# A SwiGLU feed-forward on one core: first sums of two or three weight pairs made by adding transfers, results kept in the slots of the sums

## The chip, the cores and the metric

The kernel runs on one core of a Trainium2 chip. The metric is device time in microseconds (us), the median of several runs; the lower the better. The engines are named as in the profile: PE is TensorE (matmuls; PEld is the loading of its weights, which overlaps them), DVE is VectorE, ACT is ScalarE, POOL is GpSimd and SP is SyncE. SP issues most of the transfers, POOL some of them. Data lies in HBM, is worked on in SBUF (128 partitions), and TensorE adds its products up in PSUM, in eight banks of 128 x 512 fp32.

## The reference

A decoder layer on 256 tokens of width 2048: a normalised input goes through one input projection into two groups of heads, their outputs through an output projection, and a SwiGLU feed-forward of width 5632 follows. The change touches the last step alone:

```python
def hybrid_layer(x, ..., w_out, ffn_norm_g, w_gate, w_up, w_down):
    ...
    h = x + jnp.concatenate([gla_out, nsa_out], axis=-1) @ w_out
    m = rms_norm(h, ffn_norm_g)
    return h + (jax.nn.silu(m @ w_gate) * (m @ w_up)) @ w_down
```

Here w_gate and w_up are 2048 x 5632, w_down is 5632 x 2048, all fp32.

## The kernel before

**Precision.** A product of fp32 matrices is made of three matmuls of a reduced format (fp32r): each operand is split into a high part and a low part, and high x high, high x low and low x high are added in PSUM. The split of a weight tile (`in_parts`, L660 ff) is one ScalarE instruction for the high part (L661) and one VectorE instruction for the low part (L662).

**Blocks and pairs.** The feed-forward runs over 11 blocks of 512 columns. For a block `fb`, `gate_up(fb)` multiplies the normalised tokens (two tiles of 128) with the block's columns of w_gate and w_up. The 2048 rows of these go in eight *pairs* of 128-row tiles, a and b. A plain pair is 8 products of 128 x 128 by 128 x 512, so 24 matmuls. The other kind of pair does with 7 products (21 matmuls), by Strassen's method in Winograd's form on the 2 x 2 scheme of (tokens 0, tokens 1) x (a, b) x (gate, up). A pair with 7 needs:
- three weight tiles as they are (gate a, gate b, up a), split in one go as a 128 x 1536 tile; a plain pair splits four (128 x 2048);
- a *first sum* `s1` (two tiles: gate b + up b, and up a + up b; one VectorE instruction of 128 x 1024, L1210) and a *second sum* `s2` (two tiles made from `s1`; two VectorE instructions of 128 x 512, L1211 and L1212), each then split as 128 x 1024;
- *forms* of the tokens (`pair_forms`), made once for all blocks.

The products add up in PSUM banks numbered 1 to 8. At a block's end VectorE combines them (L1238 to L1241 after a copy by ScalarE, then L1252, L1255 and L1256 with the gate's activation on ScalarE) into five result tiles `q1, u, q5u, q7u, q57u`. Bank 8 is written by plain pairs alone.

**The order of the blocks.** Block 0 is followed straight by block 1. From there on, the down product of a block (`down`, 96 matmuls) stands between the gate and up products of later blocks: `gate_up(2)`, `down(1)`, and so on, so that a block's results have the time of a down product to be turned and split. Within a block the tiles of a pair are split ahead of the matmuls that use them, and a scheduling layer places the instructions of each engine; each engine then runs its own in order.

**Where a sum comes from.** `SUMS` names pairs whose sums are made earlier, in the projection stage, as background work (`sum_rows`), and kept in DRAM. `fetch_sums` (L1168) brings them back by two POOL transfers of 512 KB, one pair ahead. For those pairs VectorE makes no sum in the block. Before the change, blocks 2 to 7 have seven pairs with 7 products and pair 6 plain, one stored pair (7); blocks 8 to 10 have eight pairs with 7 products, three of them stored (2, 5, 7).

**Slots.** Tiles come from pools of a fixed number of slots; a new tile waits until the slot's last reader is done. `g4` is the common pool of 24 slots, `fsum` holds second sums (two slots), `fraw` the weights as loaded (three slots), `ftwo` split weights (four slots), and `f2` the block results and the work tiles of the forms (six slots).

Of the kernel before, what the change touches and what calls it, by code (L numbers as in the profile page):

```python
# [8 lines left out]
F32 = mybir.dt.float32  # L9
# [6 lines left out]
P = 128  # L16
# [21 lines left out]
def kernel(  # L38
# [182 lines left out]
    done = set()  # L221
    cols = kp.tile([P, 164], F32, name="cols")
    pc = bank()
    have_rows = transpose(pc[:, 0:16], rows0[:16, :], 16)
    have_cols = nc.vector.tensor_copy(cols[:, 0:16], pc[:, 0:16])
    ag, fg, gains = cols[:, 0:16], cols[:, 16:32], cols[:, 32:36]
    cw = cols[:, 36:100].rearrange("p (i c) -> p i c", i=4)
    pos = cols[:, 100:164].rearrange("p (w j) -> p w j", w=2)
    kgain = cp.tile([P, 3], F32, name="kgain")
# [6 lines left out]
    def cols_rest():  # L236
        for _ in range(8):
            yield
        nc.gpsimd.memset(w2b, 0.0)
        with behind(last["dma"]):  # L240
            small_loads()
        for _ in range(20):
            yield
        pc = bank()
        transpose(pc[:, 0:P], rows2)
        transpose(pc[:, P:P + 20], rows[:20, :], 20)
        nc.vector.tensor_copy(cols[:, 36:164], pc[:, 0:P])
        nc.vector.tensor_copy(cols[:, 16:36], pc[:, P:P + 20])
        TS(kgain, gains[:, 1:4], gains[:, 0:1], None, ALU.mult)
        third_group(w2r, w2b, slice(32, 64))  # L250
        done.add("cols")
# [779 lines left out]

    ALL7 = 8
    FIRST7.update({f: (0, 1, 2, 3, 4, 5, 7) for f in range(2, ALL7)})

# [6 lines left out]

    def pair_forms(pair, v):


        f = g2([4, P])
        a0, a1, b0, b1 = v[:, 0, :P], v[:, 0, P:], v[:, 1, :P], v[:, 1, P:]
        TT(f[:, 0], b1, a1, ALU.subtract)
        TT(f[:, 1], f[:, 0], b0, ALU.subtract)
        TT(f[:, 2], b0, b1, ALU.subtract)
        TT(f[:, 3], a0, f[:, 1], ALU.add)  # L1050
        r = forms[pair] = g4([2, 4, P], F32R)
        in_parts(r[:, 0], r[:, 1], f)

    def late_forms():
        for pair in PAIRS7:
            if pair not in EARLY7:
                for _ in range(6):
                    yield
                v, ks = g2([2, S]), slice(2 * pair % 4, 2 * pair % 4 + 2)
                with behind(last["d"]):  # L1060
                    TT(v, f32(hT_h[pair // 2][:, ks]), f32(hT_l[pair // 2][:, ks]), ALU.add)
                    pair_forms(pair, v)

# [30 lines left out]

    SUMS = {f: (2, 5, 7) if f >= ALL7 else (7,) for f in range(2, NFB)}
    SUMS[1] = (2, 3, 4, 5)
# [26 lines left out]
    def ffn_pools():  # L1123
        nonlocal g2, small
        for pool in (wp, s2p, s1p, cp):
            pool.release()
        fr = ctx.enter_context(tc.tile_pool(name="fr", bufs=1, reuse_waits="tile"))
        fs = ctx.enter_context(tc.tile_pool(name="fs", bufs=1, reuse_waits="tile"))
        fp = ctx.enter_context(tc.tile_pool(name="fp", bufs=1, reuse_waits="tile"))
        fw["sum"] = slot(fs, "fsum", 2)  # L1130
        fw["raw"], fw["two"] = slot(fr, "fraw", 3, LINE), slot(fp, "ftwo", 4, LINE)
        g2, small = slot(fs, "f2", 6), slot(fs, "fm", 4)

# [35 lines left out]


    banks = {}

    def gate_up(fb):
# [11 lines left out]

        order, sevens = (ORDER0, ORDER1, ORDER)[0 if fb == 0 else 1 if fb < ALL7 else 2], FIRST7.get(fb, PAIRS7)
        last7 = max(sevens, key=order.index)
# [6 lines left out]
        for at, pair in enumerate(order):  # L1194
# [6 lines left out]
            if at < 7:  # L1201
                fetch_sums(fb, order[at + 1])
            r = load4([(w_gate[0], a, 2, fb * FB), (w_up[0], a, 1 if ready else 2, fb * FB)])
            if ready:
                s1, s2 = fetched.pop((fb, pair))
            if pair in sevens:
                w = parts_of(r[:, 0:3])
                if not ready:
                    s1, s2 = g4([2, 512]), fw["sum"]([2, 512])
                    TT(s1, r[:, 1:3], r[:, 3:4].to_broadcast([P, 2, 512]), ALU.add)  # L1210
                    TT(s2[:, 0], s1[:, 1], r[:, 1], ALU.add)  # L1211
                    TT(s2[:, 1], s2[:, 0], r[:, 0], ALU.add)  # L1212
# [22 lines left out]
            if pair == last7:  # L1235
                q1, u, q5u, q7u, q57u = (g2([512]) for _ in range(5))
                act(q1, banks[1], AF.Copy)
                TT(u, banks[6], q1, ALU.add)  # L1238
                TT(q5u, banks[5], u, ALU.subtract)
                TT(q7u, banks[7], u, ALU.add)  # L1240
                TT(q57u, banks[5], q7u, ALU.subtract)  # L1241
                if fb == 1:
                    urgent.append(turn_act(0, (1, 5)))
                if fb:
                    seed(0, DOWN[min(fb - 1, 1)])
# [15 lines left out]
    def turn_act(fb, qs):  # L1261
# [13 lines left out]
        if fb == NFB - 1:  # L1275
            for pair in range(2):
                yield
                yield
                v, ks = g2([2, S]), slice(2 * pair, 2 * pair + 2)
                TT(v, f32(hi[:, ks]), f32(lo[:, ks]), ALU.add)  # L1280
                pair_forms(8 + pair, v)

# [24 lines left out]
    def down_last():  # L1307
# [56 lines left out]
        ws = parts_of(load4([(w_down[0], 4 * f, 4, 1536)]))  # L1364
        q1, u, q5u, q7u, q57u = (g2([512]) for _ in range(5))
        act(q1, at[1], AF.Copy)
# [79 lines left out]
```

## Time and profile before

| what | value |
|---|---|
| median of 3 runs | 1097.95 us (1097.88 to 1098.21) |
| the profiled execution, its own time | 1100.68 us |
| its span, first to last instruction | 1098.9 us |
| granted TensorE clock | 1.00 |
| ACT busy | 755.4 us (69%) |
| matmuls of gate and up products (L1179) | 1842 recorded, 431.3 us busy |
| transfers on POOL's queue | 46.14 MB, 11.4% of 16 engines' span |
| transfers on SP's queue | 223.68 MB, 59.2% |

The profile is one execution, some us longer than the median run; a difference that the trace shows is set against the profiled execution's own time. "Busy" is the time in which an engine ran instructions. A group row gives the line, engine, operation, names (output<-inputs), shapes and count, then busy time and the mean of one, then the idle time before its instructions and what ended it.

### The profile page before, as it was taken

What the parts mean: (1) busy time and instruction counts of PE and PEld (TensorE: products, weight loads), DVE (VectorE), ACT (ScalarE), POOL (GpSimd) and SP (SyncE); (2) the same over time, 40 slices, a digit from 0 to 9 for tenths busy, and PEclk for the clock granted to TensorE, in tenths of its full rate; (3) what the DMA queues carried; (4) which work ended last, traced back from release to release, by engine and by line L of the source; (5) the groups of instructions that cost most, each with busy time, mean ns of one, the idle gap of its engine ahead of it and who ended that gap; (6) DMA issues with size and microseconds to landing.
All of it is one profiled execution on the core that took longest, in us unless ns stands there. A gap on an engine that the chain in (4) does not pass through costs nothing.

```text
span 1098.9 us, 14699 instructions
## 1 busy us (share of the span) xinstructions
PE 1092.1 (99%) x5274; PEld 899.8 (82%) x5274; DVE 993.4 (90%) x1313; ACT 755.4 (69%) x1048; POOL 79.8 (7%) x150
## 2 busy tenths in 40 slices
PE   9999999999999999999999999999999999999998
PEld 8888888987888877888878888888888888888887
DVE  5778879986899888997999999999999999999997
ACT  7755557545687587666585866768585867777785
POOL 4100001032110100100000000000000000000000
PEclk9999999999999999999999999999999999999999
DMA  7999978467877956685566657576566768677663
GB/s 278 356 371 355 378 248 296 165 226 283 307 276 253 336 183 232 226 324 172 181 231 210 213 199 252 180 253 208 209 230 205 252 216 287 212 263 235 226 230 115
DMA packets 128885, 271.22 MB, mean 247 GB/s; under 512 B 7126, under 2 KB 9210, under 8 KB 128812
## 3 DMA queue, kind: packets, MB, share of 16 engines
q1 hardware_dynamic: 115532, 223.68, 59.2%
q0 software_dynamic: 12672, 46.14, 11.4%
q8 instruction: 41, 0.67, 0.2%
q10 hardware_dynamic: 608, 0.47, 0.1%
q14 instruction: 32, 0.26, 0.1%
HBM read 247.19 MB, written 23.07 MB: 246 GB/s over the span
## 4 chain that ended last, share of the span: by engine, by line
PE 82%; DVE 8%; issue 4%; ACT 3%; POOL 2%; DMA 1%; SPq 0%; DVEq 0%; POOLq 0%; ACTq 0%
PE bank L297 39%; PE bank L1179 36%; PE bank L215 2%; PE bank L1320 2%; DVE lo L145 2%; DVE ftwo L662 1%; DMA g<-in_x_dram 1%; PE bank L977 1%; ACT hi L144 1%; POOL sm L218 1%; DMA fraw<-in_w_up_dram 1%; ACT g L912 1%; DVE g L1111 0%; DVE g L1210 0%; POOL sc L218 0%
## 5 line engine op out<-in xcount | busy, mean ns | idle before, releaser
L1179 PE MATMUL bank<-ftwo,g 128*128 128x512 f32 x1842 | 431.3, 393 | 0.5 <-ACT ftwo L661 0.2
L1179 PEld LDWEIGHTS bank<-ftwo,g 128*128 128x128 f32 x1842 | 341.0, 188 | 77.9 <-DVE ftwo L662 5.0
L297 PE MATMUL bank<-hi,g 128*128 128x512 f32 (+1 forms) x1088 | 320.9, 376 | 0.4 <-ACT g L912 0.4
L662 DVE TENSOR_TENSOR ftwo<-fraw,ftwo 128x1536 fp32r<-128x1536 f32 (+1 forms) x130 | 256.6, 1976 | 8.2 <-ACT ftwo L661 7.4
L661 ACT ACTIVATE ftwo<-fraw 128x1536 fp32r<-128x1536 f32 (+1 forms) x130 | 216.0, 1664 | 28.3 <-DMA fraw<-in_w_up_dram 18.6
L297 PE MATMUL bank<-ftwo,g 128*128 128x512 f32 x960 | 220.6, 390 | 0.0
L297 PEld LDWEIGHTS bank<-hi,g 128*128 128x128 f32 x1088 | 191.6, 188 | 30.9 <-issue 1.0
L297 PEld LDWEIGHTS bank<-ftwo,g 128*128 128x128 f32 x960 | 179.6, 188 | 38.4 <-ACT bank L1291 0.3
L297 PE MATMUL bank<-lo,g 128*128 128x512 f32 (+3 forms) x544 | 193.0, 375 | 0.1
L144 ACT ACTIVATE hi<-raw 128x1024 fp32r<-128x1024 f32 (+3 forms) x124 | 130.7, 1059 | 81.9 <-PE bank L297 62.7
L145 DVE TENSOR_TENSOR lo<-raw,hi 128x1024 fp32r<-128x1024 f32 (+3 forms) x124 | 150.2, 1218 | 33.5 <-ACT hi L144 32.9
L661 ACT ACTIVATE ftwo<-g 128x1024 fp32r<-128x1024 f32 x76 | 80.3, 1057 | 75.1 <-DVE g L1210 48.9
L297 PEld LDWEIGHTS bank<-lo,g 128*128 128x128 f32 x544 | 98.3, 189 | 14.6 <-DVE lo L145 0.3
L662 DVE TENSOR_TENSOR ftwo<-g,ftwo 128x1024 fp32r<-128x1024 f32 x76 | 92.7, 1220 | 10.5 <-ACT ftwo L661 10.5
L662 DVE TENSOR_TENSOR ftwo<-fsum,ftwo 128x1024 fp32r<-128x1024 f32 x76 | 92.6, 1219 | 0.5 <-ACT ftwo L661 0.5
L661 ACT ACTIVATE ftwo<-fsum 128x1024 fp32r<-128x1024 f32 x76 | 79.6, 1048 | 5.4 <-DVE fsum L1212 3.7
L1303 ACT COPY g<-bank 128x512 f32<-128x512 f32 x80 | 46.0, 589 | 38.3 <-PE bank L297 36.7
L1210 DVE TENSOR_TENSOR g<-fraw 128x1024 f32<-128x1024 f32 x54 | 65.2, 1219 | 0.8 <-DMA fraw<-in_w_up_dram 0.8
L1291 ACT COPY bank<-g 128x512 f32<-128x512 f32 x80 | 45.3, 594 | 15.0 <-DVE f L1240 8.4
L661 ACT ACTIVATE g<-bank 128x512 fp32r<-128x512 f32 x46 | 27.2, 598 | 30.2 <-PE bank L215 24.3
L1168 POOL DMA_DIRECT2D g<-sums x20 | 10.6, 533 | 502.0 <-DVE ftwo L662 473.4
L215 PE MATMUL bank<-ident,g 128*128 128x128 f32 (+3 forms) x232 | 42.8, 278 | 1.3 <-DVE g L863 0.9
(250 smaller groups left out, 918.5 us busy)
## 6 DMA issues: line engine op xcount, KB each, us to landing
fraw<-in_w_gate_dram SPq DMA_DIRECT2D x86, 512.0 KB, 3.9
fraw<-in_w_down_dram SPq DMA_DIRECT2D x42, 1024.0 KB, 5.0
raw<-in_w_in_dram SPq DMA_DIRECT2D x36, 1024.0 KB, 5.8
fraw<-in_w_up_dram SPq DMA_DIRECT2D x66, 512.0 KB, 4.8
sums<-g POOLq DMA_DIRECT2D x40, 512.0 KB, 6.5
raw<-in_w_out_dram SPq DMA_DIRECT2D x16, 1024.0 KB, 8.6
g<-in_w_gate_dram SPq DMA_DIRECT2D x20, 512.0 KB, 8.4
g<-in_w_up_dram SPq DMA_DIRECT2D x20, 512.0 KB, 9.3
```

Of the source, the lines that this page charges most:

```text
L144: act(h[:, i:i + n], r[:, k + i:k + i + n], AF.Copy)
L145: last["d"] = TT(o[:, i:i + n], r[:, k + i:k + i + n], f32(h[:, i:i + n]), ALU.subtract)
L215: return nc.tensor.transpose(o, i, ident[:n, :n])
L218: nc.gpsimd.tensor_tensor(o, i, mhalf[:i.shape[0], :i.shape[1]], ALU.pow)
L297: last["mm"] = mm(bk[t], a[:, k, t * P:(t + 1) * P], ws[k][m][:, off:off + w], start=(first_ and k == 0 and i == 0), stop=(end and k == 3 ...
L661: act(hi, ps, AF.Copy)
L662: last["d"] = TT(lo, ps, f32(hi), ALU.subtract)
L1179: mm(banks[q], x, m, start=todo[q] == total[q], stop=todo[q] == 1)
L1210: TT(s1, r[:, 1:3], r[:, 3:4].to_broadcast([P, 2, 512]), ALU.add)
L1291: last["seed", n] = nc.scalar.copy(banks[qs[n][t]], h_sb[n][:, t, :])
L1303: nc.scalar.copy(h_sb[n][:, t, :], bs[t])
L1320: mm(bk, u, m, start=(first and i == 0), stop=(end and i == 2), skip_group_check=onto)
```

## The change

- In blocks 2 to 7 pair 6 becomes a pair with 7 products too, and the natural order of pairs is used in all blocks from 2 on. No block from 2 on writes bank 8 in its gate and up products.
- `SUMS` stores pairs 4 and 7 for blocks 2 to 7, pair 7 alone for blocks 8 to 10: 20 pairs in all with blocks 0 and 1, as many as before.
- `HALVES`: the first sum of pairs 2 and 6 (blocks 2 to 7) or 2, 4 and 6 (blocks 8 to 10) is made by transfers: POOL loads gate b and up a (256 KB each) into the two halves of a tile of the common pool, and a third transfer adds up b to both halves (512 KB). `fetch_half` is called two pairs ahead. VectorE then makes the second sum alone, and SP loads three tiles of the pair in place of four.
- The first sum that VectorE still makes goes to a slot of `fsum`, no longer to the common pool. `fsum` has three slots, `fraw` four, `f2` one.
- The block results take up all three slots of `fsum`, two results in each. Late forms take a tile of the common pool, and the columns of small constants that only the first stages use lie in a pool that is released before the feed-forward.

```diff
...
-    ALL7 = 8
-    FIRST7.update({f: (0, 1, 2, 3, 4, 5, 7) for f in range(2, ALL7)})
+    HALVES = {f: (2, 6) if f < 8 else (2, 4, 6) for f in range(2, NFB)}
...
+    def form_tiles():
+        t = g4([2, 512])
+        return t[:, 0].rearrange("p (a b) -> p a b", a=2), t[:, 1].rearrange("p (a b) -> p a b", a=4)
...
-                v, ks = g2([2, S]), slice(2 * pair % 4, 2 * pair % 4 + 2)
+                v, f = form_tiles()
+                ks = slice(2 * pair % 4, 2 * pair % 4 + 2)
...
-    SUMS = {f: (2, 5, 7) if f >= ALL7 else (7,) for f in range(2, NFB)}
+    SUMS = {f: (4, 7) if f < 8 else (7,) for f in range(2, NFB)}
     SUMS[1] = (2, 3, 4, 5)
     SUMS[0] = (4,)
...
-        fw["sum"] = slot(fs, "fsum", 2)
-        fw["raw"], fw["two"] = slot(fr, "fraw", 3, LINE), slot(fp, "ftwo", 4, LINE)
-        g2, small = slot(fs, "f2", 6), slot(fs, "fm", 4)
+        fw["sum"] = slot(fs, "fsum", 3)
+        fw["raw"], fw["two"] = slot(fr, "fraw", 4, LINE), slot(fp, "ftwo", 4, LINE)
+        g2, small = slot(fs, "f2", 1), slot(fs, "fm", 4)
...
+    halves = {}
+
+    def fetch_half(fb, pair):
+
+        a, c = 2 * pair * P, slice(fb * FB, (fb + 1) * FB)
+        s1 = halves[fb, pair] = g4([2, 512])
+        nc.gpsimd.dma_start(s1[:, 0], w_gate[0][a + P:a + 2 * P, c])
+        nc.gpsimd.dma_start(s1[:, 1], w_up[0][a:a + P, c])
+        b = w_up[0][a + P:a + 2 * P, c].unsqueeze(1).to_broadcast([P, 2, 512])
+        nc.gpsimd.dma_start(s1, b, accum_op=ALU.add)
+
...
-        order, sevens = (ORDER0, ORDER1, ORDER)[0 if fb == 0 else 1 if fb < ALL7 else 2], FIRST7.get(fb, PAIRS7)
+        order, sevens = (ORDER0, ORDER1, ORDER)[min(fb, 2)], FIRST7.get(fb, PAIRS7)
...
             ready = row_sums.get((fb, pair))
             if at < 7:
                 fetch_sums(fb, order[at + 1])
-            r = load4([(w_gate[0], a, 2, fb * FB), (w_up[0], a, 1 if ready else 2, fb * FB)])
+            if at < 6 and order[at + 2] in HALVES.get(fb, ()):
+                fetch_half(fb, order[at + 2])
+            half = halves.pop((fb, pair), None)
+            r = load4([(w_gate[0], a, 2, fb * FB), (w_up[0], a, 1 if ready or half is not None else 2, fb * FB)])
             if ready:
                 s1, s2 = fetched.pop((fb, pair))
             if pair in sevens:
                 w = parts_of(r[:, 0:3])
                 if not ready:
-                    s1, s2 = g4([2, 512]), fw["sum"]([2, 512])
-                    TT(s1, r[:, 1:3], r[:, 3:4].to_broadcast([P, 2, 512]), ALU.add)
+                    s1, s2 = fw["sum"]([2, 512]) if half is None else half, fw["sum"]([2, 512])
+                    if half is None:
+                        TT(s1, r[:, 1:3], r[:, 3:4].to_broadcast([P, 2, 512]), ALU.add)
                     TT(s2[:, 0], s1[:, 1], r[:, 1], ALU.add)
                     TT(s2[:, 1], s2[:, 0], r[:, 0], ALU.add)
...
-                q1, u, q5u, q7u, q57u = (g2([512]) for _ in range(5))
+                (q1, q7u), (u, q5u), (q57u, _) = ((t[:, 0], t[:, 1]) for t in (fw["sum"]([2, 512]) for _ in range(3)))
                 act(q1, banks[1], AF.Copy)
                 TT(u, banks[6], q1, ALU.add)
...
```

In the changed kernel the lines have moved: L1210, L1211, L1212 are L1229, L1230, L1231; L1238 to L1241 are L1257 to L1260; L1252, L1255, L1256 are L1271, L1274, L1275; L1179 is L1194. Three places show what moves.

VectorE where block 0 ends and block 1 begins, before. `g_857_4685` and `fsum_4686` are the first and second sum of block 1's pair 0, `ftwo_4699` their split parts, `f_845` to `f_849` the results of block 0, and `bank_4397` is its bank 8:

```order
L1240 TENSOR_TENSOR f_848_4599<-bank_4482,f_846_4597 128x512
L1210 TENSOR_TENSOR g_857_4685<-fraw_4679 128x1024
L1241 TENSOR_TENSOR f_849_4600<-bank_4478,f_848_4599 128x512
L1211 TENSOR_TENSOR fsum_4686<-g_857_4685,fraw_4679 128x512
L662 TENSOR_TENSOR ftwo_4699<-g_857_4685,ftwo_4699 128x1024
L1252 TENSOR_TENSOR f_845_4596<-bank_4349,f_845_4596 128x512
L1255 TENSOR_TENSOR f_847_4598<-bank_4368,f_847_4598 128x512
L1212 TENSOR_TENSOR fsum_4686<-fsum_4686,fraw_4679 128x512
L1252 TENSOR_TENSOR f_848_4599<-bank_4385,f_848_4599 128x512
L662 TENSOR_TENSOR ftwo_4723<-fraw_4720,ftwo_4723 128x2048
L1256 SCALAR_TENSOR_TENSOR f_845_4596<-f_847_4598,rf,f_845_4596 128x512
L1255 TENSOR_TENSOR f_849_4600<-bank_4397,f_849_4600 128x512
```

The same place after the change; `fsum_4597` to `fsum_4599` hold block 0's results, `fsum_4684` and `fsum_4685` are the two sums, `bank_4398` is bank 8:

```order
L1260 TENSOR_TENSOR fsum_4599<-bank_4479,fsum_4597 128x512
L1271 TENSOR_TENSOR fsum_4597<-bank_4350,fsum_4597 128x512
L1274 TENSOR_TENSOR fsum_4598<-bank_4369,fsum_4598 128x512
L1271 TENSOR_TENSOR fsum_4597<-bank_4386,fsum_4597 128x512
L1275 SCALAR_TENSOR_TENSOR fsum_4597<-fsum_4598,rf,fsum_4597 128x512
L1274 TENSOR_TENSOR fsum_4599<-bank_4398,fsum_4599 128x512
L1229 TENSOR_TENSOR fsum_4684<-fraw_4678 128x1024
L1275 SCALAR_TENSOR_TENSOR fsum_4597<-fsum_4599,rf,fsum_4597 128x512
L1230 TENSOR_TENSOR fsum_4685<-fsum_4684,fraw_4678 128x512
L662 TENSOR_TENSOR ftwo_4698<-fsum_4684,ftwo_4698 128x1024
L1231 TENSOR_TENSOR fsum_4685<-fsum_4685,fraw_4678 128x512
L662 TENSOR_TENSOR ftwo_4722<-fraw_4719,ftwo_4722 128x2048
```

The first sum and its split stood ahead of the results' combination with the last banks, and now stand behind the read of bank 8.

TensorE at the start of block 1 after the change; `ftwo_4681` are the split raw weights of pair 0, `ftwo_4698` its split sums (a product's first matmul takes the high part), `ftwo_4722` and `ftwo_4761` the weights of the next two pairs:

```order
L1194 MATMUL bank_4464<-ftwo_4681,g_726_3983 128x512 x2
L1194 MATMUL bank_4464<-ftwo_4681,g_727_3984 128x512
L1194 MATMUL bank_4350<-ftwo_4681,g_726_3983 128x512 x2
L1194 MATMUL bank_4350<-ftwo_4681,g_727_3984 128x512
L1194 MATMUL bank_4369<-ftwo_4681,g_746_4062 128x512 x3
L1194 MATMUL bank_4479<-ftwo_4698,g_746_4062 128x512
L1194 MATMUL bank_4483<-ftwo_4698,g_746_4062 128x512
L1194 MATMUL bank_4479<-ftwo_4698,g_746_4062 128x512 x2
L1194 MATMUL bank_4483<-ftwo_4698,g_746_4062 128x512 x2
L1194 MATMUL bank_4350<-ftwo_4722,g_726_3983 128x512
L1194 MATMUL bank_4369<-ftwo_4722,g_726_3983 128x512
L1194 MATMUL bank_4398<-ftwo_4722,g_726_3983 128x512
```

Nine matmuls need the raw weights alone, then six need the first sum; behind these rows follow one of the third pair's (`ftwo_4761`), two of the second sum's high part, and eight more of `ftwo_4722` before the second sum's low part is used.

POOL in block 9 after the change; `g_1272`, `g_1285` and `g_1295` are the first sums of pairs 2, 4 and 6, and the waits are those that the instruction itself has:

```order
L1181 DMA g_1272_8345<-in_w_gate_dram 128x512 [waits DMASW6_49,DVE_49]
L1182 DMA g_1272_8345<-in_w_up_dram 128x512
L1184 DMA g_1272_8345<-in_w_up_dram 128x2x512 [waits DMASW2_49,DMASW1_49]
L1181 DMA g_1285_8437<-in_w_gate_dram 128x512 [waits PE_49]
L1182 DMA g_1285_8437<-in_w_up_dram 128x512
L1181 DMA g_1295_8513<-in_w_gate_dram 128x512 [waits DMASW3_49,DVE_49]
L1182 DMA g_1295_8513<-in_w_up_dram 128x512 [waits DMASW7_49]
L1184 DMA g_1285_8437<-in_w_up_dram 128x2x512 [waits DMASW5_49,DMASW4_49,DMASW0_49]
```

The two loads of pair 6 stand between the loads of pair 4 and the transfer that adds to them, and the first of the two waits for VectorE.

More of the change, by code (lines that the diff above doesn't have):

```diff
@@ L221 @@
     done = set()
-    cols = kp.tile([P, 164], F32, name="cols")
+    cols, cols2 = kp.tile([P, 36], F32, name="cols"), cp.tile([P, 128], F32, name="cols2")
     pc = bank()
@@ L226 @@
     ag, fg, gains = cols[:, 0:16], cols[:, 16:32], cols[:, 32:36]
-    cw = cols[:, 36:100].rearrange("p (i c) -> p i c", i=4)
-    pos = cols[:, 100:164].rearrange("p (w j) -> p w j", w=2)
+    cw = cols2[:, 0:64].rearrange("p (i c) -> p i c", i=4)
+    pos = cols2[:, 64:128].rearrange("p (w j) -> p w j", w=2)
     kgain = cp.tile([P, 3], F32, name="kgain")
@@ L246, in cols_rest @@
         transpose(pc[:, P:P + 20], rows[:20, :], 20)
-        nc.vector.tensor_copy(cols[:, 36:164], pc[:, 0:P])
+        nc.vector.tensor_copy(cols2, pc[:, 0:P])
         nc.vector.tensor_copy(cols[:, 16:36], pc[:, P:P + 20])
@@ L1040, with pair_forms @@
     turned = set()
-    def pair_forms(pair, v):
-        f = g2([4, P])
+    def pair_forms(pair, v, f=None):
+        f = g2([4, P]) if f is None else f
         a0, a1, b0, b1 = v[:, 0, :P], v[:, 0, P:], v[:, 1, :P], v[:, 1, P:]
@@ L1058, in late_forms @@
                     yield
-                v, ks = g2([2, S]), slice(2 * pair % 4, 2 * pair % 4 + 2)
+                v, f = form_tiles()
+                ks = slice(2 * pair % 4, 2 * pair % 4 + 2)
                 with behind(last["d"]):
                     TT(v, f32(hT_h[pair // 2][:, ks]), f32(hT_l[pair // 2][:, ks]), ALU.add)
-                    pair_forms(pair, v)
+                    pair_forms(pair, v, f)
     def turn_h(n, hi, lo):
@@ L1278, in turn_act @@
                 yield
-                v, ks = g2([2, S]), slice(2 * pair, 2 * pair + 2)
+                (v, f), ks = form_tiles(), slice(2 * pair, 2 * pair + 2)
                 TT(v, f32(hi[:, ks]), f32(lo[:, ks]), ALU.add)
-                pair_forms(8 + pair, v)
+                pair_forms(8 + pair, v, f)
     DOWN = ((6, 7), (2, 3), (6, 7), (4, 8)), ((1, 6), (7, 5), (2, 3), (4, 1))
@@ L1364, in down_last @@
         ws = parts_of(load4([(w_down[0], 4 * f, 4, 1536)]))
-        q1, u, q5u, q7u, q57u = (g2([512]) for _ in range(5))
+        (q1, q7u), (u, q5u), (q57u, _) = ((t[:, 0], t[:, 1]) for t in (fw["sum"]([2, 512]) for _ in range(3)))
         act(q1, at[1], AF.Copy)
```

## The prediction

> **What bounds the kernel now.** I read the page's first block, then the chain of waits over the feed-forward part, then a table of windows with one row for each block's repeat, and last the waits of TensorE itself. The page gives busy times by engine:
>
> ```profile
> span 1098.9 us, 14699 instructions
> ...
> PE 1092.1 (99%) x5274; PEld 899.8 (82%) x5274; DVE 993.4 (90%) x1313; ACT 755.4 (69%) x1048; POOL 79.8 (7%) x150
> ...
> PEclk9999999999999999999999999999999999999999
> ```
>
> TensorE is busy 99% of the span at full clock. The chain (start, length, what) says the same of the feed-forward part; three of its pieces are a stretch from before block 0's end to block 1's, then one repeat of a middle block (the rest of the gate and up products, then the 96 of the down product), and one of block 8:
>
> ```profile
> 423.71 68.72 PE bank L1179 x300
> ...
> 587.26 32.90 PE bank L1179 x144
> 620.16 21.83 PE bank L297 x96
> ...
> 896.79 32.28 PE bank L1179 x141
> ```
>
> A matmul costs 32.90/144 = 0.2285 us. TensorE's own waits from 424 us to the end, and those of its weight loads in one middle block, are
>
> ```profile
> PE bank L1179 <- ACT ftwo L661: 0.2, 1, 0.2
> ...
> PEld bank L1179 <- DVE ftwo L662: 0.3, 1, 0.3
> ```
>
> So nothing holds TensorE, but VectorE is close behind it: a weight load already waits 0.3 us for a low part. The windows (length, then busy time of PE, PEld, DVE, ACT, POOL, clock, DMA share, GB/s) show how close, for a middle block and for blocks 8, 9, 10:
>
> ```profile
> 641.99:703.89 61.90, 61.90 (x277) 50.57 (x276) 60.87 (x57) 44.26 (x48) 1.06 (x2) 1.00 0.64 217
> ...
> 889.61:950.87 61.26, 61.26 (x273) 49.95 (x273) 59.63 (x55) 45.82 (x49) 3.18 (x6) 1.00 0.72 245
> 950.87:1012.20 61.33, 61.33 (x273) 49.98 (x273) 60.06 (x55) 45.73 (x49) 3.18 (x6) 1.00 0.73 244
> 1012.20:1074.41 62.21, 62.21 (x281) 50.73 (x281) 59.42 (x63) 48.32 (x55) 2.11 (x4) 1.00 0.67 223
> ```
>
> The rule that follows: a matmul taken out of blocks 2 to 10 is a gain, VectorE work is free up to about 1.2 us a block, and any stall of TensorE after 424 us is a loss in full, because no idle time follows in which it could be made up.
>
> **Term 1, TensorE.** Pair 6 of blocks 2 to 7 turns from 8 products into 7: 3 matmuls less in each of 6 blocks. By the pitch that is 18 x 0.2285 = 4.1 us. By the windows a block without a plain pair is 61.90 - 61.33 = 0.57 to 61.90 - 61.26 = 0.64 us shorter, 3.4 to 3.8 us for six. I take **-3.8**.
>
> **Term 2, VectorE.** These are its groups in that middle block (count, then busy sum and mean ns):
>
> ```profile
> L662 DVE TENSOR_TENSOR ftwo<-fraw,ftwo 128x1536 fp32r<-128x1536 f32 x7 | 12.3, 1755 | 0.1
> L662 DVE TENSOR_TENSOR ftwo<-fraw,ftwo 128x2048 fp32r<-128x2048 f32 x5 | 11.4, 2286 | 0.0
> L662 DVE TENSOR_TENSOR ftwo<-g,ftwo 128x1024 fp32r<-128x1024 f32 x7 | 8.5, 1219 | 0.8 <-ACT ftwo L661 0.8
> L1210 DVE TENSOR_TENSOR g<-fraw 128x1024 f32<-128x1024 f32 x6 | 7.2, 1219 | 0.0
> L1211 DVE TENSOR_TENSOR fsum<-g,fraw 128x512 f32<-128x512 f32 x7 | 4.8, 686 | 0.1
> ...
> L1255 DVE TENSOR_TENSOR f<-bank,f 128x512 f32<-128x512 f32 x2 | 1.4, 686 | 0.0
> ```
>
> Back to back, each starts about 0.08 us before the one ahead of it ends (below: 447.27 + 1.22 = 448.49, the next starts at 448.40), so each costs its duration less 0.08. In a middle block the low part of one 128x2048 becomes one of 128x1536 (-2.20 + 1.67), two more 128x1024 low parts come (+2.28), two first sums go (-2.28: of eight pairs two are now stored and two added by transfers, four are left), the second sums stay at twelve, and the last L1255 goes with the plain pair (-0.60): -1.1 us, so 59.7 of about 61.3. That is the balance that blocks 8 and 9 have today without a wait. In blocks 8 to 10 one first sum goes (-1.14), and since stored pairs 2 and 5 brought their second sums along, four L1211/L1212 come back (4 x 0.60): **+1.26**, so 60.9 and 61.3 of 61.3. VectorE is then as long as TensorE there. I count this at 0: what covers it is the idle time of 1.63 and 1.27 us. If the cover is gone, it costs 0 to 1 us a block.
>
> **Term 3, the boundary between blocks 0 and 1.** No down product stands here, so block 1's first sums are made while block 0 ends. VectorE, then ScalarE, in the profile before (start, length):
>
> ```profile
> 447.27 1.22 DVE L1210 TENSOR_TENSOR g<-fraw 128x1024 f32<-128x1024 f32 x1
> 448.40 0.68 DVE L1241 TENSOR_TENSOR f<-bank,f 128x512 f32<-128x512 f32 x1
> 449.00 0.68 DVE L1211 TENSOR_TENSOR fsum<-g,fraw 128x512 f32<-128x512 f32 x1
> 449.69 1.23 DVE L662 TENSOR_TENSOR ftwo<-g,ftwo 128x1024 fp32r<-128x1024 f32 x1
> ...
> 451.66 0.69 DVE L1255 TENSOR_TENSOR f<-bank,f 128x512 f32<-128x512 f32 x1
> 452.26 0.68 DVE L1212 TENSOR_TENSOR fsum<-fsum,fraw 128x512 f32<-128x512 f32 x1
> ...
> 456.49 0.69 DVE L1255 TENSOR_TENSOR f<-bank,f 128x512 f32<-128x512 f32 x1
> ```
>
> ```profile
> 448.60 1.06 ACT L661 ACTIVATE ftwo<-g 128x1024 fp32r<-128x1024 f32 x1 [5.54 <-DVE g L1210]
> 449.56 1.90 ACT L661 ACTIVATE ftwo<-fraw 128x2048 fp32r<-128x2048 f32 x1
> ...
> 455.32 1.47 ACT L661 ACTIVATE ftwo<-fraw 128x1536 fp32r<-128x1536 f32 x1
> ```
>
> Before, pair 0's first sum went to a tile of the common pool at 447.27 and both its parts were done by 450.9. Now it needs a slot of the sums, and block 0's results hold all three. The order puts L1229 (L1210 before) behind the second L1274 (L1255 before), which reads bank 8, the last that block 0 fills. Block 0 ends 132 matmuls after 423.71, at 132 x 68.72/300: 453.95. With 0 to 0.4 us for the release I take 454.2, an estimate. Then L1274 to 454.8, the first sum 454.8 to 456.0, its high part on ScalarE 456.1 to 457.2, its low part on VectorE 457.2 to 458.4: 7.5 us later than before. Queued behind it: on ScalarE the high parts of 128x2048 (457.1 to 459.0), 128x1536 (to 460.4) and of the second sum (to 461.4); on VectorE the second sum and its low part, which end about 463.
>
> TensorE reaches 456.0 on nine matmuls of the raw part, which is ready. It waits 1.2 for the high part, issues two, waits about 0.75 for the low part, issues four and then three of the next pair (460.0), waits 0.4 for the 128x1536 and, one matmul on, 0.75 for the second sum's high part: 1.2 + 0.75 + 0.4 + 0.75 = **+3.1** us; 0.2 us earlier or later at the release moves it to 2.9 or 3.3, and a filler that I mis-ordered would make it 2.4 to 4. The end of the low part at 463 is met by the eight matmuls in between. Nothing of it returns, by the rule above. At later boundaries the 21.83 us of a down product lie between the results and the next first sum, so the same wait costs nothing there.
>
> **Term 4, the added transfers.** Middle blocks issue 10 instead of 2 transfers on POOL, blocks 8 to 10 issue 11 instead of 6, each at 0.53 us on an engine that is 3 us busy in a block. Traffic: a first sum by transfers moves 1 MB and saves 256 KB on SP's queue. A middle block gets 3 x 0.77 MB on 217 GB/s x 61.9 us = 13.4 MB, so a share of 0.64 becomes about 0.75, next to the 0.73 that block 9 carries without a wait. In middle blocks the two added pairs lie four apart and I find over 15 us between the issue and the need, so 0. The close place is pair 4 of blocks 8 to 10. Rows of block 9 before, and what a stored sum of the same 512 KB takes to land on this queue, and 1 MB on SP's:
>
> ```profile
> 958.27 1.22 DVE L662 TENSOR_TENSOR ftwo<-g,ftwo 128x1024 fp32r<-128x1024 f32 x1
> ...
> 967.96 1.22 DVE L1210 TENSOR_TENSOR g<-fraw 128x1024 f32<-128x1024 f32 x1
> ```
>
> ```profile
> 959.78 0.53 POOL L1168 DMA_DIRECT2D g<-sums  x1 [32.74 <-DVE ftwo L662]
> ...
> DMA to landing us min/median/max: 3.4/4.2/6.3
> ...
> fraw<-in_w_down_dram SPq DMA_DIRECT2D x24, 1024.0 KB, 5.1
> ```
>
> POOL is in order, and the second load of pair 6 stands ahead of pair 4's adding transfer and waits for the slot of pair 2, which is free when pair 2's first low part ends, about 959.4. Two issues later the adding transfer goes out, about 960.6. VectorE asks for pair 4's first sum about 967.0 (967.96 less the first sum that it no longer makes). **The window is 6.4 us.** No row shows an adding transfer. If it is like a plain one, 4.2 fits; if it moves each byte twice, 1 MB on SP's queue took 5.1 and twice the median is 8.4. I take 0, as the nearest rows (3.4 to 6.3) lie inside; the far end is 2.0 us late, 6 us over three blocks, less up to 0.5 us a block of slack.
>
> The Trainium skill, "Collectives: The Full Stack", section "The bandwidth ceiling: the fold count and why AG ≠ RS ≠ AR", says that an adding copy is slower because it "needs two source reads" on one ring, at about half the rate of a plain one. By that the adding transfer would take up to the far end above, and the sum would be 1101 to 1103 us; no run here shows it yet.
>
> Everything else costs 0: ahead of the feed-forward part the order of the instructions is the same on all engines, the same 20 pairs are stored, and the late forms only change their tile.
>
> **Sum.** -3.8 + 3.1 + 0 + 0 = -0.7. Against the profiled execution's own 1100.68 us (span 1098.9 and 1.8 around it) that is 1100.0. That execution lies 2.73 over the median of 1097.95, so on the median's scale I forecast **1097.3**.
>
> **The rivals.**
> - *A, the forecast:* the removed matmuls are given back at the 0-1 boundary: 1097.95 - 4.1 + 2.9 to 1097.95 - 3.4 + 4 = 1096.7 to 1098.5. Chance 0.44.
> - *B, no stall at the boundary:* the release comes sooner or TensorE's order has work that I overlooked. For it: only a few us are in question. Against it: the order itself. 1097.95 - 4.1 = 1093.8 to 1094.5. Chance 0.22.
> - *C, the adding transfer is late in blocks 8 to 10:* it decides once landing takes over 6.4 to 6.9 us. Priced at 1.5 to 2 us a block: 1097.3 + 4.5 to 1097.3 + 6 = 1101.8 to 1103.3, less with one block alone (1099 to 1100). Against it: the rows 3.4 to 6.3. For it: 6.3 touches the window. Chance 0.27.
> - *D, VectorE becomes the bound in blocks 8 to 10:* it decides if 1.26 us exceed the idle time that is of use, and gives 0.5 to 1 us a block, 1098.8 to 1100.3. Chance 0.07.
>
> **How the numbers follow.** 0.2% of this time is 2.2 us, about what a measurement can tell from no change: 1095.75 to 1100.15. B is faster, with a small tail of A: 0.23. A without it, D and the mild third of C are the same: 0.43 + 0.06 + 0.09, so 0.58. The rest of C is slower, with a tail of D on top of A: 0.19. The range takes in most of B and most of C: 1093.9 to 1102.0; A's own is 1096.7 to 1098.5.
>
> **What would show it.** Right: 18 matmuls fewer on L1194, middle blocks of 61.3 us in the windows; a gap of TensorE of about 3 us in several pieces between 456 and 462, released by ScalarE and VectorE on ftwo, with L1229 starting about 455. Wrong: that L1229 starts near 447, or that gap is under 1 us (B); weight loads in blocks 8 to 10 that wait for the adding transfer through VectorE (C), or for VectorE with no idle time in it (D). Gaps in middle blocks would overturn terms 2 and 4.

## The result, and the profile after

The changed kernel takes **1106.51 us** (median of 6 runs, 1104.73 to 1107.07); the kernel before took 1098.26 us in the runs beside it (6 runs, 1097.88 to 1099.68). The ratio is 1.0069, 95% interval 1.0056 to 1.0082: slower by about 8 us, outside the range that was forecast. The page after begins

```profile
span 1105.1 us, 14839 instructions
...
PE 1091.6 (99%) x5256; PEld 896.5 (81%) x5256; DVE 989.8 (90%) x1316; ACT 764.7 (69%) x1060; POOL 129.2 (12%) x213
...
q0 software_dynamic: 21744, 68.17, 20.2%
```

TensorE has 18 matmuls less and is 0.5 us less busy, while the span is 6.2 us longer: TensorE now waits. POOL's queue moves 68.17 MB in place of 46.14 and takes 20.2% of the transfer engines' time in place of 11.4%. The chain of waits (start, length, what) shows where:

```profile
453.30 1.15 DVE fsum L1229
455.51 2.12 ACT ftwo L661 x2
...
648.75 31.82 PE bank L1194 x139
...
895.93 8.01 DMA g<-in_w_up_dram
...
960.13 8.12 DMA g<-in_w_up_dram
...
1025.03 8.58 DMA g<-in_w_up_dram
```

The chain no longer runs through TensorE alone. It leaves it once where block 1 begins, and once in each of blocks 8, 9 and 10, there for a transfer of up b that takes 8 us, which is the adding transfer. Between these places it is TensorE without a gap. In block 8 ScalarE, VectorE and TensorE read, behind that transfer (in brackets the idle time before, and what ended it):

```profile
904.03 1.06 ACT L661 ACTIVATE ftwo<-g 128x1024 fp32r<-128x1024 f32 x1 [3.84 <-DMA g<-in_w_up_dram]
905.00 1.04 ACT L661 ACTIVATE ftwo<-fsum 128x1024 fp32r<-128x1024 f32 x1
...
906.07 1.23 DVE L662 TENSOR_TENSOR ftwo<-fsum,ftwo 128x1024 fp32r<-128x1024 f32 x1 [1.36 <-ACT ftwo L661]
...
906.09 0.73 PE L1194 MATMUL bank<-ftwo,g 128*128 128x512 f32 x2 [1.36 <-ACT ftwo L661]
907.35 1.89 PE L1194 MATMUL bank<-ftwo,g 128*128 128x512 f32 x7 [0.53 <-DVE ftwo L662]
```

ScalarE stood 3.84 us for the first sum of pair 4. Behind it, in ScalarE's order, came the high part of pair 3's second sum, which VectorE had ready at 901.45; TensorE waited for the two parts of that sum. The windows of a middle block, of blocks 8 and 9, and of block 10's repeat (columns as before, in brackets the number of instructions) give the sizes:

```profile
641.14:702.34 61.20, 61.20 (x273) 49.97 (x273) 59.51 (x56) 45.77 (x49) 6.83 (x10) 1.00 0.79 258
...
885.94:949.70 63.76, 61.87 (x271) 49.16 (x271) 60.53 (x58) 45.52 (x49) 8.09 (x11) 1.00 0.83 247
949.70:1015.57 65.87, 63.74 (x275) 51.46 (x275) 61.55 (x58) 46.40 (x50) 8.07 (x11) 0.97 0.80 240
1015.57:1079.00 63.43, 61.42 (x274) 48.77 (x273) 59.62 (x64) 47.04 (x53) 5.79 (x8) 1.00 0.71 224
```

With block 2's start at 518.18 before and 518.82 after, the two profiled executions compare stage by stage like this:

| stretch | before | after | difference |
|---|---|---|---|
| start to the first gapless matmul of block 0 | 423.71 | 421.96 | -1.75 |
| from there to block 2 | 94.47 | 96.86 | +2.39 |
| blocks 2 to 7 | 371.43 | 367.12 | -4.31 |
| blocks 8 and 9 | 122.59 | 129.63 | +7.04 |
| block 10 and the end | 86.70 | 89.53 | +2.83 |

I take the first row as no part of the change: the order of instructions there is the same, and the profiled execution of before lay 2.73 us over its own median. The other four rows add up to +7.95 us, against 8.25 between the medians. So blocks 8 to 10 lost 9.9 us, and that is the result.

### The profile page after: what moved, and what is told of

It is laid out like the page before. It is cut to its first block, busy times and chain, and to the rows that moved or that the text cites. A ratio compares the mean times of both kernels' runs of the same rounds, so it can differ in the third digit from the quotient of the medians.

```text
span 1105.1 us, 14839 instructions
## 1 busy us (share of the span) xinstructions
PE 1091.6 (99%) x5256; PEld 896.5 (81%) x5256; DVE 989.8 (90%) x1316; ACT 764.7 (69%) x1060; POOL 129.2 (12%) x213
## 3 DMA queue, kind: packets, MB, share of 16 engines
q0 software_dynamic: 21744, 68.17, 20.2%
## 4 chain that ended last, share of the span: by engine, by line
PE 58%; DMA 2%; DVE 2%; ACT 2%; issue 1%; POOL 0%; ACTq 0%; DVEq 0%; POOLq 0%
PE bank L1194 34%; PE bank L297 21%; DMA g<-in_w_up_dram 2%; PE bank L1339 2%; PE bank L215 1%; DVE ftwo L662 1%; ACT ftwo L661 1%; DVE g L662 0%; DVE lo L145 0%; ACT g L1079 0%; POOL g L1182 0%; ACT hi L144 0%; POOL g L1181 0%; DVE fsum L1230 0%; DVE fsum L1231 0%
## 5 line engine op out<-in xcount | busy, mean ns | idle before, releaser
L1194 PE MATMUL bank<-ftwo,g 128*128 128x512 f32 x1824 | 431.1, 394 | 8.4 <-ACT ftwo L661 6.2
L1194 PEld LDWEIGHTS bank<-ftwo,g 128*128 128x128 f32 x1824 | 338.2, 188 | 88.5 <-ACT ftwo L661 11.4
L662 DVE TENSOR_TENSOR ftwo<-fraw,ftwo 128x1536 fp32r<-128x1536 f32 (+1 forms) x130 | 252.4, 1947 | 4.6 <-ACT ftwo L661 4.3
L661 ACT ACTIVATE ftwo<-fraw 128x1536 fp32r<-128x1536 f32 (+1 forms) x130 | 212.2, 1641 | 15.5 <-PE bank L1194 14.2
L661 ACT ACTIVATE ftwo<-fsum 128x1024 fp32r<-128x1024 f32 x121 | 125.0, 1054 | 78.4 <-DVE fsum L1229 59.3
L662 DVE TENSOR_TENSOR ftwo<-fsum,ftwo 128x1024 fp32r<-128x1024 f32 x121 | 145.4, 1218 | 18.9 <-ACT ftwo L661 18.9
L661 ACT ACTIVATE ftwo<-g 128x1024 fp32r<-128x1024 f32 x43 | 45.5, 1058 | 32.9 <-PE bank L1194 19.7
L662 DVE TENSOR_TENSOR ftwo<-g,ftwo 128x1024 fp32r<-128x1024 f32 x43 | 52.4, 1218 | 0.9 <-ACT ftwo L661 0.8
L1119 POOL DMA_DIRECT2D sums<-g x40 | 21.8, 546 | 259.2 <-DVE g L1115 205.5
L1229 DVE TENSOR_TENSOR fsum<-fraw 128x1024 f32<-128x1024 f32 x39 | 47.5, 1217 | 0.1
L1231 DVE TENSOR_TENSOR fsum<-fsum,fraw 128x512 f32<-128x512 f32 x60 | 41.2, 687 | 1.0
```

Source lines behind the costliest of these rows:

```text
L661: act(hi, ps, AF.Copy)
L662: last["d"] = TT(lo, ps, f32(hi), ALU.subtract)
L1194: mm(banks[q], x, m, start=todo[q] == total[q], stop=todo[q] == 1)
```

## The experiments

All are edits of the changed kernel. Two suspects came from the trace: the adding transfer of pair 4 (L), and VectorE's 1.26 us more in the same blocks (V). At the boundary the suspect is the first sum's slot (S).

**The order on POOL.** The addition waits for its pair's two loads, and POOL holds it behind the next pair's loads. The edit has the two loads of a pair issued behind the addition of the pair before (`behind`):

```diff
+        with behind(last.get("add")):
-        nc.gpsimd.dma_start(s1[:, 0], w_gate[0][a + P:a + 2 * P, c])
-        nc.gpsimd.dma_start(s1[:, 1], w_up[0][a:a + P, c])
+            nc.gpsimd.dma_start(s1[:, 0], w_gate[0][a + P:a + 2 * P, c])
+            nc.gpsimd.dma_start(s1[:, 1], w_up[0][a:a + P, c])
...
-        nc.gpsimd.dma_start(s1, b, accum_op=ALU.add)
+        last["add"] = nc.gpsimd.dma_start(s1, b, accum_op=ALU.add)
```

> Edit: each first load of a pair's first sum is issued on POOL only behind the adding transfer of the pair before it, so that in blocks 8 to 10 the addition for pair 4 no longer stands behind the loads for pair 6. Theory L (the adding transfer of pair 4 lands late): in block 8 it was issued at 895.93, held up by the load for pair 6 that waited for VectorE until 894.6, and landed at 903.93 where VectorE and ScalarE asked for it about 900.4 to 901. Its own loads are down about 892, so it goes out some 3.5 us sooner and lands about 900.0 to 900.5: TensorE's waits in blocks 8 to 10 fall from 6.0 us to under 1.5 and the three blocks lose 0 to 2 us in place of 9.9: 1097 to 1099.5 us. Theory V (VectorE, 1.26 us longer in these blocks, is the bound there): the order on POOL makes no difference, 1106 us.

Measured: **1099.24 us** (ratio to before 1.0002, 0.9993 to 1.0011), 7.3 us less than the changed kernel, at the upper end of what L gave. POOL's timeline in block 8, of the changed kernel and then of this one (start, length, what, and the idle time before with its releaser):

```profile
894.87 0.54 POOL L1181 DMA_DIRECT2D g<-in_w_gate_dram  x1 [7.49 <-DVE ftwo L662]
895.40 0.54 POOL L1182 DMA_DIRECT2D g<-in_w_up_dram  x1
895.93 1.27 POOL L1184 DMA_DIRECT2D g<-in_w_up_dram  x1
```

```profile
892.65 1.23 POOL L1185 DMA_DIRECT2D g<-in_w_up_dram  x1 [4.37 <-DMA g<-in_w_up_dram]
895.76 0.58 POOL L1182 DMA_DIRECT2D g<-in_w_gate_dram  x1 [1.88 <-DVE ftwo L662]
```

In the changed kernel POOL stood 7.49 us on the load for pair 6, and the addition that was ready went out at 895.93, 10.0 us into the block (885.94). Now it goes out at 892.65, 5.8 us into a block that starts at 886.83. Blocks 8 and 9 take

```profile
886.83:948.60 61.77, 61.77 (x273) 49.59 (x273) 60.80 (x58) 46.08 (x49) 8.16 (x11) 1.00 0.81 255
948.60:1010.35 61.75, 61.73 (x273) 49.58 (x273) 60.71 (x58) 46.10 (x49) 8.14 (x11) 1.00 0.81 256
```

and TensorE has no wait in them. VectorE does the same work; V alone is refuted. What is left over the middle blocks' 61.20 is 0.55 to 0.57 us each.

**What makes the transfer long.** The same transfer, with nothing added:

```diff
-        nc.gpsimd.dma_start(s1, b, accum_op=ALU.add)
+        nc.gpsimd.dma_start(s1, b)
```

> Edit: the third transfer of each first sum copies up b into both halves and adds nothing (the first sums of pairs 2, 4 and 6 are then wrong: this kernel leaves that addition out). Same bytes from the same rows by the same three issues. If it is the addition that makes the transfer long: issue 0.55 us in place of 1.22, landing 4 to 5 us in place of 8.6, no wait in blocks 8 to 10, about 1098 us. If it is the source that is read twice, or the busy transfer engines (0.80 of their time): landing stays 7 to 9 us and the time 1105 to 1107 us.

Measured: 1098.66 us in one run, with no wait of TensorE in blocks 8 to 10. The rows of that line (duration in ns min/median/max, first and last start, then us from issue to landing), of the changed kernel and then of this one:

```profile
L1184 POOL DMA_DIRECT2D g<-in_w_up_dram x21: 1192/1221/1754, 485.7 to 1025.8; - x21
...
DMA to landing us min/median/max: 6.1/8.6/11.0
```

```profile
L1184 POOL DMA_DIRECT2D g<-in_w_up_dram x21: 712/712/728, 486.2 to 1020.0; - x21
...
DMA to landing us min/median/max: 4.0/4.8/6.6
```

It is the addition that costs: 1.22 us to issue in place of 0.71 (0.55 was expected), and 8.6 us to land in place of 4.8, with the same 68.17 MB on POOL's queue and the same source read twice. With the addition the queue has 21744 packets in place of 19056, which is 128 more for each of the 21 transfers, and a middle block keeps the transfer engines busy for 0.80 of its time in place of 0.73, at the same 257 to 258 GB/s. So the fuller engines are part of what the addition brings; they alone make little: the stored sums of 512 KB land after a median of 5.8 and 5.1 us in the changed kernel (common pool and `fsum`), against 3.8 and 4.6 before the change. Here the transfer goes out 10.0 us into block 8, behind pair 6's loads as in the changed kernel, and still lands in time. Both causes are needed: an early long one is in time, and so is a late short one.

**VectorE makes pair 4's first sum.**

```diff
-    HALVES = {f: (2, 6) if f < 8 else (2, 4, 6) for f in range(2, NFB)}
+    HALVES = {f: (2, 6) for f in range(2, NFB)}
```

> Edit: pair 4 of blocks 8 to 10 has its first sum made by VectorE again; two pairs by transfers in every block from 2 on. Theory L: no transfer is late any more, so the 9.9 us of blocks 8 to 10 go, but VectorE gets 3 x 1.14 us; as it then has 62.0 to 62.4 us of work for 61.3 us of matmuls, the blocks are bound by it and lose 0.7 to 1.1 us each: 1098.5 to 1100.5 us. Theory V: VectorE was the bound already, so another 1.14 us a block comes on top: 1108 to 1110 us.

Measured: **1110.20 us** (1.0092, 1.0069 to 1.0115), slower than the changed kernel, just above what V had, and not L. Blocks 8 and 9:

```profile
887.09:952.40 65.31, 62.57 (x274) 49.73 (x274) 62.21 (x60) 46.08 (x49) 5.80 (x8) 1.00 0.72 229
952.40:1020.10 67.70, 64.00 (x273) 50.74 (x272) 62.03 (x59) 46.35 (x49) 5.79 (x8) 0.97 0.72 222
```

VectorE's 62.2 us of work explain a block of 62 us, not one of 65.3: neither theory gives that. TensorE's largest wait here is for a copy of ScalarE into a bank ahead of the down product, 5.1 us in two waits, behind a load of w_down that landed 11 us after its slot came free. A third theory was needed, and the next runs brought it into view.

**The first sums of block 1.** Both sums of its first pair go to the common pool:

```diff
-                    s1, s2 = fw["sum"]([2, 512]) if half is None else half, fw["sum"]([2, 512])
+                    to = g4 if fb == 1 and at == 0 else fw["sum"]
+                    s1, s2 = to([2, 512]) if half is None else half, to([2, 512])
```

> Edit: the two sums of block 1's first pair go to tiles of the common pool, as the first sum did before the change; all else as in the changed kernel. Theory S (the first sum waits for the slots that block 0's results hold): VectorE starts it about 6 us sooner, as in the profile before, TensorE's 2.1 us of waits between 453 and 460 go, and the stretch from block 0 to block 2's start falls from 96.9 to 94.5 us: 1104.1 us. Rival: the stretch is longer for another reason (the third slot of the sums or the loads of stored sums): 1106.5 us, the same as the changed kernel.

Measured: **1103.87 us** (1.0040, 1.0027 to 1.0053), 2.6 us less. In the changed kernel, TensorE's timeline at the boundary and VectorE's read

```profile
455.65 0.73 PE L1194 MATMUL bank<-ftwo,g 128*128 128x512 f32 x2 [1.05 <-ACT ftwo L661]
457.01 2.33 PE L1194 MATMUL bank<-ftwo,g 128*128 128x512 f32 x8 [0.62 <-DVE ftwo L662]
459.78 4.60 PE L1194 MATMUL bank<-ftwo,g 128*128 128x512 f32 x19 [0.44 <-ACT ftwo L661]
```

```profile
452.61 0.69 DVE L1274 TENSOR_TENSOR fsum<-bank,fsum 128x512 f32<-128x512 f32 x1
453.21 1.22 DVE L1229 TENSOR_TENSOR fsum<-fraw 128x1024 f32<-128x1024 f32 x1
```

With the edit the chain has no gap there:

```profile
422.10 68.71 PE bank L1194 x300
```

S holds: the first sum came right behind the read of bank 8, and three waits of 2.1 us in all were the price.

**Both mended.** Two of the edits above together, POOL's order and block 1's sums.

> Edit: both at once, POOL's order (each addition ahead of the next pair's loads) and block 1's first two sums in the common pool. If the two faults are separate terms, they add: 1099.24 less the 2.6 us that the second took off the changed kernel, 1096.6 us, and TensorE has no wait over 0.3 us after 424 us. Blocks 8 to 10 stay at about 61.75 us each, 0.5 over the middle blocks, since VectorE is still at the end of its budget there. If the faults covered one another, it stays at 1098.5 to 1099.2 us.

Measured: **1095.67 us** (0.9975, 0.9965 to 0.9985), faster than both kernels. The second edit took off another 3.6 us (2.6 alone), so the faults add. Blocks 8 and 9:

```profile
882.98:944.70 61.72, 61.72 (x273) 49.60 (x273) 60.75 (x58) 46.06 (x49) 8.16 (x11) 1.00 0.82 256
944.70:1006.47 61.77, 61.77 (x273) 49.63 (x273) 60.77 (x58) 46.09 (x49) 8.14 (x11) 1.00 0.81 256
```

**More stored sums.** Two runs with block 1's sums mended: pair 4 of blocks 8 to 10 stored (`SUMS` (4, 7) and `HALVES` (2, 6) in all blocks from 2 on), and those blocks as before the change (`SUMS` (2, 5, 7), no `HALVES`).

> Edit: pair 4 of blocks 8 to 10 is stored (23 stored pairs in place of 20), two pairs by transfers in every block from 2 on, block 1's first two sums in the common pool. VectorE then has 59.5 us in blocks 8 to 10 as in the middle blocks. Theory (VectorE near its limit is what keeps blocks 8 to 10 at 61.75 us after the order on POOL is mended): all nine blocks take 61.2 us, 1.6 us less than with both edits, so 1095.0 us, if three more background sums of some 2.7 us of VectorE each find room in the projection stage; 1095 to 1100 if they don't. Rival (the traffic of the transfers makes them longer): blocks 8 to 10 stay near 61.7 us, 1096.6 us or more.

> Edit: blocks 8 to 10 as before the change (pairs 2, 5 and 7 stored, no transfer that adds), the middle blocks as changed, block 1's first two sums in the common pool; 26 stored pairs. It prices what is left of the change: 18 matmuls less and no fault, 1098.4 - 4.3 = 1094.1 us, plus what six more background sums cost in the projection stage (0 to 5 us; nothing shows it yet).

Measured: 1097.75 us (0.9990, 0.9981 to 0.9999) and **1114.95 us** (1.0149, 1.0135 to 1.0163). In the first, a late block is as long as a middle one,

```profile
895.94:957.14 61.20, 61.20 (x274) 50.04 (x273) 59.52 (x56) 45.77 (x50) 6.83 (x10) 1.00 0.80 257
```

so the last 0.55 us there go with VectorE's load, and not with the traffic (0.80 as well). They lie in the down product, in the chain (start, length, what) first of the kernel with both mended, then of this one:

```profile
922.52 22.18 PE bank L297 x96
```

```profile
927.73 21.76 PE bank L297 x96
```

In the first, weight loads of the down products of blocks 8 to 10 wait for VectorE's low parts (1.2 us in three) and for ScalarE's copies (0.8 us in three); in the second there are no such waits. This edit takes out pair 4's adding transfer as well, but the addition is not it: with plain copies the blocks took 61.78 and 61.72 us. But three more background sums cost more than the 1.6 us that three blocks gain: the gapless run of matmuls starts at 427.40, against 421.98 with both mended. In the second kernel six of them delay it further (431.46), and the late blocks are long, which I had not expected:

```profile
898.11:961.98 63.87, 62.59 (x273) 49.42 (x273) 59.80 (x54) 45.67 (x49) 3.17 (x6) 1.00 0.69 234
```

VectorE is busy for 59.80 of 63.87 us: it has time, and it waits, 4.1 us in four places for a high part of ScalarE. These blocks' pairs are those of the kernel before, which took 61.3 us. What differs within such a block is where things lie: first sums in the slots of the sums, and results in the same three slots. That is the third theory (F): two pairs in a row that need two slots each make VectorE and ScalarE take turns. Its rival (W) is that VectorE's work alone makes such blocks long.

**The slots of the sums.** In blocks 8 to 10 the first sums of VectorE go to the common pool (with block 1's sums mended), once on top of the 1110.2 us kernel and once on top of the 1114.95 us one:

```diff
-                    s1, s2 = fw["sum"]([2, 512]) if half is None else half, fw["sum"]([2, 512])
+                    to = g4 if fb == 1 and at == 0 else fw["sum"]
+                    s1, s2 = (g4 if fb > 7 else to)([2, 512]) if half is None else half, to([2, 512])
```

> Edit: as the kernel in which VectorE makes pair 4's first sum again in blocks 8 to 10 (1110.2 us), but there the first sums that VectorE makes lie in the common pool, as before the change, and so do the two sums of block 1's first pair (worth 2.6 us: 1107.6 us is the base). VectorE has the same 62.2 us of work a block. Theory W (its work over the 61.2 us of matmuls is what made those blocks 65 to 68 us): 1106.5 to 1108 us. Theory F (the three slots of the sums are too few when two or three pairs in a row need two slots each, so that VectorE and ScalarE take turns): the blocks fall to what VectorE's work gives, about 62.2 us each, 1095.67 + 3 x 0.5 = 1097.2 us, range 1096 to 1099.

> Edit: as the kernel with blocks 8 to 10 as before the change (1114.95 us), but there the first sums that VectorE makes lie in the common pool. VectorE was busy 59.8 us of 63.87 in such a block. Theory F (slots): blocks 8 and 9 take 61.3 us as in the kernel before, 5 us or more off a run of 1115. If the slots are not it: 63.8 us, the same time.

Measured: **1099.47 us** (1.0008, 0.9997 to 1.0018), 8.1 us off its base of 1107.6 us and 0.5 above the range that F gave, and 1107.90 us in one run. Block 8 of each:

```profile
883.00:945.90 62.90, 62.23 (x274) 49.85 (x273) 62.54 (x60) 45.90 (x50) 5.75 (x8) 1.00 0.75 238
```

```profile
897.58:958.88 61.30, 61.30 (x273) 49.98 (x273) 60.09 (x55) 45.64 (x49) 3.18 (x6) 1.00 0.71 245
```

The slots are it in both: 61.30 us in place of 63.87 with VectorE's work nearly the same (60.09 us), and 62.90 in place of 65.31, of which VectorE is now busy for 62.54 and waits for nothing. The turns show in VectorE's waits for ScalarE, 0.8 us in one place where they were 4.1 in four. The 1110.2 us were slots first and VectorE second.

**The same on the best kernel.** If slots still cost there, the 0.55 us would go.

> Edit: both mended (POOL's order, block 1's first two sums in the common pool; 1095.67 us), and in blocks 8 to 10 the first sums that VectorE makes lie in the common pool too. These blocks take 61.7 to 61.8 us there, 0.5 over the middle ones. Theory F (turns for the three slots of the sums): 61.2 to 61.3 us each, 1094.1 us. Theory W (VectorE's work, 60.7 us of 61.2, leaves too little slack): no change, 1095.7 us.

Measured: **1111.14 us** (1.0121, 1.0104 to 1.0137), a clear miss of both theories. POOL's load for pair 4 in block 8, of the kernel with both mended and then of this one:

```profile
883.28 0.58 POOL L1182 DMA_DIRECT2D g<-in_w_gate_dram  x1 [21.82 <-PE bank L297]
...
891.91 0.58 POOL L1182 DMA_DIRECT2D g<-in_w_gate_dram  x1 [1.76 <-DVE ftwo L662]
```

```profile
886.38 0.58 POOL L1182 DMA_DIRECT2D g<-in_w_gate_dram  x1 [25.11 <-DVE ftwo L662]
...
900.80 0.58 POOL L1182 DMA_DIRECT2D g<-in_w_gate_dram  x1 [7.77 <-DVE ftwo L662]
```

Block 8 starts at the same time in both to within 0.1 us, so pair 4's load goes out 3.1 us later and pair 6's 8.9 us later. The adding transfers draw their tiles from the same common pool, and with more first sums in it their loads wait for VectorE to free a slot; TensorE waits 10.7 us for low parts, and its clock falls twice (last section). So in the late blocks the changed kernel's choice, first sums in the slots of the sums, is the better one as long as three pairs come by transfers. I read it so that these stand between the pairs that need two slots; no run shows that by itself, nor whether slots still cost anything there.

## Why the prediction was wrong

**Blocks 8 to 10 (term 4) is the step that failed.** It named the place, POOL's order and the window, and took 0 for the price, since plain transfers landed within 3.4 to 6.3 us. The adding transfer landed after a median of 8.6 us, and after 8.0, 8.1 and 8.6 us in these three places, beyond the plain rows and near the far end of 8.4 that the text had put down for a transfer that moves each byte twice. The time of issue held: 10.0 us into block 8 (the text had 9.7), though it was the first of pair 6's loads that waited, not the second. TensorE's waits were 1.9, 2.1 and about 2 us, as rival C had priced a block. The value should have been taken from the other end: no row showed an adding transfer, so the nearest row was no evidence that it is like a plain one. The Trainium skill's rule in "Collectives: The Full Stack" ("The bandwidth ceiling: the fold count and why AG ≠ RS ≠ AR"), by which the addition reads two sources at about half the rate, pointed to the right end, though the section states it for the reduce step of a ring of cores. The ratio of 8.6 to 4.8 us for the same transfer without the addition agrees with it; no trace here shows the two reads themselves.

The window of 6.4 us was too wide as well: it asked when VectorE needs the sum. ScalarE splits it first, and with POOL's order mended, where nothing is late, it does so 15.5 us into block 8. That leaves 5.5 us from an issue at 10.0.

**Rival C was the case, and its top of 1103.3 was too low by 3.2 us.** It priced blocks 8 to 10 at 6 us at most, and TensorE's waits there are 6.0 us, but the blocks lost 9.9. VectorE's 1.26 us (rival D) account for about 1.3 of the rest, at 0.44 and 0.46 us a block against before (61.72 and 61.77 with both mended, 61.26 and 61.33 before); I had counted the two as alternatives, and they add. In the profiled execution TensorE's clock also fell after one of the waits, which cost 1.7 us (last section), and 0.8 us are not placed. The clock does not explain the median, though: of the six runs three have a mean clock of 0.997 or 0.998 (1105.27 to 1106.85 us) and three one of 1.000 (1104.73 to 1107.07 us). What lengthens those three by as much stays open.

**Term 1** held and was a little small: -4.31 us in place of -3.8, with blocks of 61.20 us. **Term 2**: 59.51 us of VectorE in a middle block where 59.7 was forecast, and 60.75 in a late one with both mended where 60.9 to 61.3 was, with no idle time of use left: the cost of 0.45 lies inside the 0 to 1 us that was written for it, and 0 was the wrong value. The share of the transfer engines in a middle block came out at 0.80 in place of 0.75, without a wait. **Term 3** held in its mechanism: L1229 stood behind the read of bank 8, at 453.21 in an execution whose block 0 starts 1.75 us sooner, so 7.7 us later than before where 7.5 was forecast. The stretch grew by 2.4 us, of which 2.1 are waits, where I had +3.1: the first two waits were 1.05 and 0.62 (1.2 and 0.75 in the text), and after the low part one of 0.44 stood where I had two of 0.4 and 0.75.

**What I did not see** is that the changed layout has no reserve in slots. A first and a second sum of a pair fill two of three slots, so what looked like a budget of VectorE is also an order of pairs: full pairs must not stand side by side in blocks without slack. What this costs in the changed kernel itself no run separates. It made the obvious repair (VectorE makes the sum again) slower than the fault, 1110.20 us against 1106.51.

## What to carry to other kernels

Price an operation that the trace doesn't hold from its far end when it stands on a path without slack, and let the range hold the sum of the rivals that can come together. Take its deadline from the engine that asks first, which here was ScalarE and not VectorE. On an engine that issues transfers in order, look for what stands ahead of the one that is needed first: three lines of order were worth 7 us here. A tile moved to another pool changes who waits for whom twice, where it goes and where it came from, so try both ends before calling the engine the bound.

## What the runs showed of the hardware

TensorE's granted clock fell to half after two short waits with matmuls between them. In block 9 of the changed kernel (windows as before):

```profile
968.00:970.00 2.00, 0.94 (x5) 0.44 (x3) 0.69 (x1) 1.51 (x2) 0.00 (x0) 1.00 0.96 265
...
971.00:972.00 1.00, 0.47 (x3) 0.20 (x2) 1.00 (x2) 0.87 (x1) 0.00 (x0) 0.94 1.10 262
972.00:973.00 1.00, 1.00 (x3) 0.81 (x4) 1.00 (x2) 0.62 (x1) 0.00 (x0) 0.50 0.87 201
...
974.00:975.00 1.00, 1.00 (x4) 0.75 (x3) 1.00 (x1) 0.00 (x0) 0.57 (x1) 0.50 0.85 295
975.00:976.00 1.00, 1.00 (x5) 0.81 (x4) 1.00 (x2) 0.00 (x0) 0.00 (x0) 0.85 1.06 414
```

From 971.9 to 975.3 it stood at 0.50, 3.4 us, which cost 1.7 us: block 9 is 2.1 us longer than block 8 (65.87 and 63.76), though its waits are only 0.2 us longer. In block 8 the clock stayed at 1.00 through a wait of nearly the same shape (1.4 and 0.5 us, here 1.6 and 0.5).

The Trainium skill, "TensorE: Matmul & The Clock Gate", section "🔬 Part 1: The HAM clock gate (the "warmup" mystery)", has the clock set by a free-running window of about 3.4 us, so that when a transition comes depends on where in the window the work lands. The traces agree with that, while the section's table, which has the clock fall after an idle window, does not cover a window that is partly busy.

In all the traces of this case the clock falls seven times ahead of the last matmuls, in six of the kernels. Each fall lasts 3.41 us, but for one of 6.83, twice that. In the last kernel above (1111.14 us) two falls begin 68.27 us apart, 20 times 3.413. In the changed kernel, counted in steps of 3.413 us from where its clock first stands at 1.00, TensorE was busy for 37% of the step that ends where the clock falls in block 9, and for 54% and 52% of the steps that hold most of the waits of blocks 8 and 10. Counted in the same way, the seven falls came after steps in which it was busy for 3, 7, 10, 15, 15, 37 and 46% of the time. No fall came after a step of 47% or more, and one step of 45%, ahead of the feed-forward part, brought none either. So the busy share of such a step tells most of it, and what decides near 45% stays open; no run was made to test it.
